# The first norm's weights as one row spread by TensorE, and the first row tile taken alone through all weight blocks

## The chip, the cores and the metric

The kernel runs on one NeuronCore of a Trainium2 chip. The metric is the device time of one launch in microseconds. The kernel before took 1310.49 us, the median of three runs (1310.32 to 1311.75). The engines go by the profile's names: PE is TensorE, DVE is VectorE, ACT is ScalarE, POOL is GpSimd, SP is SyncE, which issues most of the transfers.

## The reference

One layer of a decoder trunk over 1040 rows (16 learned meta tokens ahead of 1024 of the sequence), 1024 wide: a norm, a wide projection, an HGRN2 recurrence beside a causal pooling, a merge by gates, a projection, a residual, then a gated MLP with a causal convolution. Only its beginning matters here:

```python
def rmsnorm(x, gain):
    xf = x.astype(jnp.float32)
    y = xf * lax.rsqrt(jnp.mean(xf * xf, axis=-1, keepdims=True) + EPS)
    return (y * gain.astype(jnp.float32)).astype(x.dtype)
...
u = rmsnorm(h, mix_norm_pre[l])
proj = u @ w_in[l]
q, f_logit, i_in, g_out, v_pool, gate_a, gate_b = jnp.split(proj, cuts, axis=-1)
```

`i_in`, 512 columns wide, is the value input v of the recurrence. All is float32.

## The kernel before, in words

Every float32 operand of a large product is cut into a high part (a cast to the fast format float32r, on ScalarE) and a low part (operand less high part, on VectorE), and a product is three: high by high, high by low, low by high.

The opening computes v for nine row tiles: eight of 128 rows and one of the 16 meta tokens, in the order 1, 5, 2, 6, 3, 7, meta, 4, 8. This document numbers them by that order from 0. Four weight blocks of 256 x 512 (two k-steps of 128 each, so k = 0, 1 lie in block 0 and k = 6, 7 in block 3) hold the columns of `i_in`. They are loaded into `wiraw` and split once, by `split_wi`, into `whi`, `wlo` (`wihi`, `wilo` for the last). The steps of one row tile are:

- `norm_steps`: ScalarE squares the row with a sum and takes the root (`un`, `std`); VectorE takes the inverse (`rstd`) and then multiplies row, inverse and gains in two halves of 512 columns (L410). The gains `g1` must lie in all 128 partitions.
- `feature_steps`, once for each half: TensorE transposes four blocks of 128 x 128 into a PSUM bank `pt` (L421), ScalarE casts it to `uhi`, VectorE subtracts to `ulo`. The first half gives k = 0 to 3, the second k = 4 to 7.
- `v_mm`: three products for each k onto the tile's bank `pv` (L187 to L189), 128 x 512 each: 24 for a tile.

Before all that TensorE runs `warm(14)`, products of ones with the identity whose result nobody reads. A float32 product that isn't in the fast format shows in the trace as two instructions.

`manual_schedule` makes the written order the order of ScalarE, VectorE and TensorE in this part: each engine takes its instructions strictly in that order, so a waiting instruction holds up all behind it. SP and POOL take theirs in an order that a scheduler chooses; each load of SP also waits for the load eight before it. Tiles 0 and 1 are written out by hand; tiles 2 to 8 follow in a loop where `v_feat(i + 2)` and `v_norm(i + 4)` run ahead of the products.

`gain_bc` loads the gains into all partitions: one transfer of 512 KB that reads the same 4 KB row for each partition. On POOL, right after the identity and the ones, two kinds of masks for the heads are built: the base mask (`mtmp`, L573 to L580) and four level masks (`mt`, L583 to L591). They are first used some 330 us later.

Of the kernel before, what the change touches and what calls it, by code (L numbers as in the profile page):

```python
# [14 lines left out]
P = 128  # L15
# [54 lines left out]
def trunk_kernel(ctx: ExitStack, tc: tile.TileContext, x, meta_tokens, mix_norm_pre,  # L70
# [48 lines left out]
    def small(shape, name, tag, bufs=4):  # L119
        return sm.tile(shape, F32, tag=tag, name=nm(name), bufs=bufs)  # L120
# [7 lines left out]
    open_pool("ps", 8, PSUM)  # L128


    eps_t = const.tile([P, 1], F32, name="eps_t")
    dve.memset(eps_t, EPS)
    act.activation(small([P, 1], "std", "ns"), eps_t, AF.Sqrt)
    ident = const.tile([P, P], F32, name="ident")
    make_identity(nc, ident)
# [5 lines left out]
    def gain_bc(src, name):  # L141
        t = slot(D, name=name)
        nc.sync.dma_start(t, src[0].partition_broadcast(P))
        return t
# [304 lines left out]
    def load_wi(j):  # L449
        raw = slot(1024, name="wiraw")  # L450
        nc.sync.dma_start(raw.rearrange("p (k c) -> p k c", k=2), wblock(WIN, 2 * j, 2, CI, 512))
        return raw
# [1 line left out]

    vtiles = [row_tiles[i] for i in (1, 5, 2, 6, 3, 7, 0, 4, 8)]
    rows_in = [load_row(*vtiles[0])]
    g1 = gain_bc(mix_norm_pre, "g1")
    raws = [load_wi(0)]
    rows_in.append(load_row(*vtiles[1]))
    raws += [load_wi(j) for j in range(1, 4)]  # L460
    rows_in += [load_row(*rt) for rt in vtiles[2:]]

    prow = slot(P, name="prow")
# [106 lines left out]
    mbase = const.tile([P, SB], U8, name="mbase")  # L570
    mtmps = slot(P + len(LEVELS) * P // 2, name="mtmps")
    mtmp = mtmps[:, :P]
    pool_e.memset(mtmp, 1.0)  # L573
    pool_e.affine_select(out=mtmp, in_=mtmp, compare_op=ALU.is_ge, fill=0.0, base=0,
                         pattern=[[-2, P // 2], [0, 2]], channel_multiplier=1)
# [450 lines left out]
    vb = [bank("pv") for _ in range(2)]  # L1026
    E = mybir.EngineType
    with tc.manual_schedule(engines={E.Activation, E.DVE, E.PE}):
        warm(14)
        n0, n1 = (norm_steps(rows_in[i], P, g1) for i in range(2))  # L1030
        next(n0)
        next(n0)
        un0 = next(n0)
        f0 = feature_steps(un0, P, uhi, ulo, vtiles[0][0])
        split_wi(raws[0])
        next(f0)
        next(f0)
        next(f0)
        next(n1)
        next(f0)  # L1040
        next(n1)
        un1 = next(n1)
        v_mm(vb[0], vtiles[0][0], 0)
        v_mm(vb[0], vtiles[0][0], 1)
        split_wi(raws[1])
        f1 = feature_steps(un1, P, uhi, ulo, vtiles[1][0])
        next(f1)
        next(f1)
        split_wi(raws[2])
        next(f1)  # L1050
        next(f1)
        split_wi(raws[3])
        for i, j in ((0, 1), (1, 0), (0, 2), (1, 1), (0, 3), (1, 2), (1, 3)):
            for k in (2 * j, 2 * j + 1):
                v_mm(vb[i], vtiles[i][0], k)
        v_norm(2)
        v_norm(3)
        for i in range(2):
            v_feat(2 + i)
            v_norm(4 + i)  # L1060
        for i in range(2):
            v_out(vb[i], vtiles[i][0])
        for i in range(2, len(vtiles)):
            ps = bank("pv")
            for k in range(KD):
                v_mm(ps, vtiles[i][0], k)
            if i < 5:
                v_feat(i + 2)
            if i == 5:
                v_feat(7)  # L1070
                v_feat(8)
            v_norm(i + 4)
            if i == 3:
                params()
            if i == 5:
                for q in ("t2", "t1", "t3", "t4"):
                    two_halves(gq, q, NM)
                sums = [gate_steps(d) for d in ds]
            if i == len(vtiles) - 1:
                with tc.issue_after(loaded_row[-1].ins):  # L1080
                    gl = Loader([job("G", h)[:2] + (P,) for h in range(EARLY_G)])
            for j in SUMS_AT.get(i, ()):
                next(sums[j], None)
            v_out(ps, vtiles[i][0])
        gates.load_first(0)
        gates.load_first(1)
        gates.ahead(2)
        for h in range(EARLY_G):
            src, n_k, xs, chunks, post = job("G", h)
            r = proj(None, 0, n_k, xs, chunks, ws=gl.next(), name="pg", by_bank=2 * h)  # L1090
            if h == EARLY_G - 1:
                post(r)
            for j in SUMS_AT.get(9 + 2 * h, ()):
                next(sums[j], None)
            if h < EARLY_G - 1:
                post(r)
            if h == 0:
                dve.tensor_tensor(vm_hl[:NM], vm_hl[:NM], vm_low[:NM], ALU.add)
                nc.sync.dma_start(vmd, vm_hl[:NM])
                gates.load_first(2)  # L1100
                gates.ahead(4)
            for j in SUMS_AT.get(10 + 2 * h, ()):
                next(sums[j], None)

        close_pool("ps")
        open_pool("pf", 4, PSUM)
        gates.load_first(3)
        for e in range(0, EARLY, 2):
            p = gates.start_pair(e)
            for f in [f[i] for i in range(2) for f in p]:  # L1110
                f()
                for j in SUMS_AT.get(13, ()) if e == 0 else ():
                    next(sums[j], None)
# [701 lines left out]
```

## Time and profile before

| | |
|---|---|
| median of three runs | 1310.49 us |
| profiled execution | 1311.92 us |
| its span, first to last instruction | 1310.2 us |
| granted TensorE clock | 0.996 |
| TensorE busy | 1291.0 us, 99% of the span |
| VectorE, ScalarE, POOL busy | 963.7, 524.4, 355.4 us |

A row of a timeline reads: start and length in us from the span's start, engine, source line, operation, output and inputs by the program's names, partitions x elements, how many instructions were merged, and in brackets how long the engine had been idle and what ended that. In a row of windows the pairs in front of the clock are busy time and instructions of TensorE and of its weight loads. Ends of matmuls are modelled, so a length is longer than the distance to the next one.

### The profile page before, as it was taken

Reading aid. Unit: us, or ns where it says so; the run is one execution under the profiler, and the core shown is the slowest. Engines: PE = TensorE matmul, PEld = TensorE weight load, DVE = VectorE, ACT = ScalarE, POOL = GpSimd, SP = SyncE. Lnnn points to the kernel's source line nnn. Section 1 sums busy time; section 2 is a strip of 40 time slices with the busy share of each in tenths; the row PEclk is TensorE's granted clock in tenths of the full one; section 3 lists DMA queues with packets and bytes.
Section 4 is the critical chain, followed back from the end, with each engine's and each line's share of the span. In section 5 each row is a group of like instructions: output and inputs, shape, how many; then the busy total and the mean of one; then the engine's idle time right before and its main releaser. Section 6 shows DMA issues by size and latency. Waiting matters only on the chain.

```text
span 1310.2 us, 21958 instructions
## 1 busy us (share of the span) xinstructions
PE 1291.0 (99%) x8650; PEld 1139.6 (87%) x8650; DVE 963.7 (74%) x1296; ACT 524.4 (40%) x905; POOL 355.4 (27%) x307
## 2 busy tenths in 40 slices
PE   8999999999999898999999999999999999999998
PEld 7799899999999898978898888888888888888886
DVE  6768965454776877765588999888998985455758
ACT  5554533332245546236564222322222332444443
POOL 3015333130000000150045555553655652000000
PEclk9999999999999999999999999999999999999999
DMA  8135542325523776876677777658776799666644
GB/s 276 42 106 166 196 160 100 118 90 158 171 73 126 238 248 203 300 223 241 239 259 242 205 203 189 170 181 209 155 179 163 155 266 289 209 225 225 228 172 161
DMA packets 143801, 247.62 MB, mean 189 GB/s; under 512 B 11000, under 2 KB 75164, under 8 KB 143698
## 3 DMA queue, kind: packets, MB, share of 16 engines
q1 hardware_dynamic: 127026, 213.42, 48.7%
q0 software_dynamic: 12064, 24.38, 11.2%
q10 hardware_dynamic: 4608, 8.41, 1.7%
q8 instruction: 68, 1.11, 0.3%
q14 instruction: 35, 0.29, 0.1%
HBM read 174.11 MB, written 95.09 MB: 205 GB/s over the span
## 4 chain that ended last, share of the span: by engine, by line
PE 95%; ACT 2%; DVE 2%; DMA 1%; issue 1%; SPq 0%; DVEq 0%; ACTq 0%
PE P L307 17%; PE P L308 17%; PE P L310 17%; PE pd L187 5%; PE pd L189 5%; PE pd L188 5%; PE pm L187 2%; PE pm L188 2%; PE pm L189 2%; PE ppv L207 1%; PE ppv L211 1%; PE ppv L208 1%; PE pv L188 1%; PE pv L187 1%; PE pv L189 1%; PE pg L207 1%
## 5 line engine op out<-in xcount | busy, mean ns | idle before, releaser
L308 PE MATMUL P<-v,whi 128*128 128x512 f32 (+2 forms) x408 | 140.7, 353 | 0.0
L307 PE MATMUL P<-v,whi 128*128 128x512 f32 (+2 forms) x408 | 140.7, 352 | 0.0
L310 PE MATMUL P<-v,wlo 128*128 128x512 f32 (+2 forms) x424 | 135.1, 349 | 0.0
L278 POOL TENSOR_TENSOR swa<-wraw,wraw 128x512 f32<-128x512 f32 x32 | 49.2, 1539 | 192.1 <-DMA wraw<-in_ffn_w_gate_dram 73.9
L252 ACT CAST whi<-wraw 128x512 fp32r<-128x512 f32 x90 | 53.1, 618 | 102.2 <-PE P L308 87.2
L1525 DVE TENSOR_TENSOR rot<-wraw,rot 128x1024 fp32r<-128x1024 f32 x31 | 37.9, 1224 | 72.3 <-ACT rot L1524 72.3
L307 PEld LDWEIGHTS P<-v,whi 128*128 128x128 f32 x408 | 76.7, 188 | 10.5
L308 PEld LDWEIGHTS P<-v,whi 128*128 128x128 f32 x408 | 76.6, 188 | 10.2
L310 PEld LDWEIGHTS P<-v,wlo 128*128 128x128 f32 x424 | 74.0, 188 | 10.8
L189 PE MATMUL pd<-rot 128*128 128x512 f32 x274 | 82.5, 388 | 0.0
L188 PE MATMUL pd<-rot 128*128 128x512 f32 x274 | 82.5, 388 | 0.0
L187 PE MATMUL pd<-rot 128*128 128x512 f32 x274 | 81.9, 388 | 0.1
L253 DVE TENSOR_TENSOR wlo<-wraw,whi 128x512 fp32r<-128x512 f32 x86 | 74.4, 887 | 2.7 <-ACT whi L252 2.7
L252 ACT CAST whi<-swa 128x512 fp32r<-128x512 f32 x64 | 38.1, 619 | 90.3 <-PE P L308 79.9
L253 DVE TENSOR_TENSOR wlo<-swb,whi 128x512 fp32r<-128x512 f32 x64 | 65.5, 1030 | 8.9 <-ACT whi L252 8.7
L1524 ACT CAST rot<-wraw 128x1024 fp32r<-128x1024 f32 x31 | 32.7, 1054 | 90.8 <-PE pd L189 89.4
L307 PE MATMUL P<-uhi,whi 128*128 128x258 f32 (+2 forms) x240 | 68.5, 303 | 0.0
L308 PE MATMUL P<-ulo,whi 128*128 128x258 f32 (+2 forms) x240 | 68.4, 303 | 0.0
L252 ACT CAST whi<-swb 128x512 fp32r<-128x512 f32 x64 | 38.1, 618 | 70.8 <-PE P L308 57.9
L307 PE MATMUL P<-t4h,whi 128*128 128x258 f32 (+2 forms) x228 | 65.5, 304 | 0.0
L308 PE MATMUL P<-t4l,whi 128*128 128x258 f32 (+2 forms) x228 | 65.3, 304 | 0.0
L307 PE MATMUL P<-t2h,whi 128*128 128x258 f32 (+2 forms) x228 | 65.3, 304 | 0.1
(388 smaller groups left out, 3844.1 us busy)
## 6 DMA issues: line engine op xcount, KB each, us to landing
wraw<-in_w_in_dram SPq DMA_DIRECT2D x36, 512.0 KB, 4.6
yt<-ysum SPq DMA_DIRECT2D x33, 512.0 KB, 5.7
wraw<-in_ffn_w_gate_dram SPq DMA_DIRECT2D x26, 512.0 KB, 7.1
wraw<-in_ffn_w_up_dram SPq DMA_DIRECT2D x22, 512.0 KB, 5.2
wsum<-in_ffn_w_down_dram SPq DMA_DIRECT2D x22, 512.0 KB, 8.6
wraw<-in_w_out_dram SPq DMA_DIRECT2D x18, 512.0 KB, 4.3
ysum<-ys SPq DMA_DIRECT2D x11, 768.0 KB, 5.0
sa<-sscr SPq DMA_DIRECT2D x16, 513.0 KB, 5.7
```

Source lines behind the costliest of these rows:

```text
L187: pe.matmul(ps, ahi, bhi, start=first, stop=False)
L188: pe.matmul(ps, ahi, blo, start=False, stop=False)
L189: pe.matmul(ps, alo, bhi, start=False, stop=last)
L207: pe.matmul(ps[:, :n], whi[:, k, :], xhi, start=(k == 0), stop=False)
L252: act.copy(hi, src)
L253: (pool_e if 4 <= i < 2 * self.early else dve).tensor_tensor(lo, src, rr(hi), ALU.subtract)
L278: pool_e.tensor_tensor(s1, a21, a22, ALU.add)
L307: pe.matmul(d, whi[:, k, :], xh[:, c : c + w], start=(k == 0 and onto is None), stop=False, **go)
L308: pe.matmul(d, whi[:, k, :], xl[:, c : c + w], start=False, stop=False, **go)
L310: pe.matmul(x[:, o : o + w], wlo[:, k, :], xh[:, c : c + w], start=False, stop=(k == 3), **go)
L1524: act.copy(hi, src)
L1525: dve.tensor_tensor(lo, src, rr(hi), ALU.subtract)
```

## The change

The gains of the first norm are no longer loaded into all partitions. A single row of 4 KB is loaded by a transfer that ScalarE issues as its first instruction; two products of a column of ones with that row (128 x 512 each) put it into all partitions of two PSUM banks; VectorE copies the first half to `g1`, ScalarE the second. Three warm-up products stay of fourteen. SP's second load is now weight block 0, and weight block 1 goes ahead of tile 1's row.

The hand-written order of tiles 0 and 1 is another. Tile 0's second half of the norm follows its first products, and tile 0 goes through all four blocks before tile 1's first transposes; tile 1 then does four k-steps behind each of its halves.

On POOL the base mask begins with a copy of one element from `prow`, a tile of parameters loaded later, so that it is built after that load has landed; the level masks, which wait for nothing, then come first.

```diff
+    gain_row, ones_row = slot(D, name="grow"), slot(P, name="ones")
+    nc.scalar.dma_start(gain_row[:1], mix_norm_pre)
     eps_t = const.tile([P, 1], F32, name="eps_t")
     dve.memset(eps_t, EPS)
+    dve.memset(ones_row[:1], 1.0)
...
     rows_in = [load_row(*vtiles[0])]
-    g1 = gain_bc(mix_norm_pre, "g1")
-    raws = [load_wi(0)]
+    g1 = slot(D, name="g1")
+    raws = [load_wi(0), load_wi(1)]
     rows_in.append(load_row(*vtiles[1]))
-    raws += [load_wi(j) for j in range(1, 4)]
+    raws += [load_wi(j) for j in range(2, 4)]
...
     mtmp = mtmps[:, :P]
+    pool_e.tensor_copy(mtmp[:1, :1], prow[:1, :1])
     pool_e.memset(mtmp, 1.0)
...
-        warm(14)
+        warm(3)
+        gps = [bank("pg1") for _ in range(2)]
+        for j in range(2):
+            pe.matmul(gps[j], ones_row[:1], gain_row[:1, j * 512 : (j + 1) * 512], start=True, stop=True)
+        dve.tensor_copy(g1[:, :512], gps[0])
         n0, n1 = (norm_steps(rows_in[i], P, g1) for i in range(2))
         next(n0)
-        next(n0)
         un0 = next(n0)
+        split_wi(raws[0])
+        act.copy(g1[:, 512:], gps[1])
         f0 = feature_steps(un0, P, uhi, ulo, vtiles[0][0])
-        split_wi(raws[0])
         next(f0)
         next(f0)
+        for k in range(2):
+            v_mm(vb[0], vtiles[0][0], k)
+        next(n0)
+        split_wi(raws[1])
         next(f0)
-        next(n1)
         next(f0)
+        for k in range(2, 4):
+            v_mm(vb[0], vtiles[0][0], k)
+        split_wi(raws[2])
+        for k in range(4, 6):
+            v_mm(vb[0], vtiles[0][0], k)
         next(n1)
         un1 = next(n1)
-        v_mm(vb[0], vtiles[0][0], 0)
-        v_mm(vb[0], vtiles[0][0], 1)
-        split_wi(raws[1])
+        split_wi(raws[3])
+        for k in range(6, 8):
+            v_mm(vb[0], vtiles[0][0], k)
         f1 = feature_steps(un1, P, uhi, ulo, vtiles[1][0])
         next(f1)
+        next(n1)
         next(f1)
-        split_wi(raws[2])
+        for k in range(4):
+            v_mm(vb[1], vtiles[1][0], k)
         next(f1)
         next(f1)
-        split_wi(raws[3])
-        for i, j in ((0, 1), (1, 0), (0, 2), (1, 1), (0, 3), (1, 2), (1, 3)):
-            for k in (2 * j, 2 * j + 1):
-                v_mm(vb[i], vtiles[i][0], k)
+        for k in range(4, 8):
+            v_mm(vb[1], vtiles[1][0], k)
```

How that moves instructions is seen best on three stretches. The first is the start of TensorE's queue before (pt_225 and pt_232 are the halves of tile 0, pt_258 and pt_269 those of tile 1):

```order
L499 MATMUL pj_127<-ident,onesm_84 128x128 x14
L421 MATMUL pt_225<-ident,un_213 128x128 x4
L421 MATMUL pt_232<-ident,un_213 128x128 x4
L187 MATMUL pv_194<-whi_221,uhi_88 128x512
L188 MATMUL pv_194<-wlo_222,uhi_88 128x512
L189 MATMUL pv_194<-whi_221,ulo_89 128x512
L187 MATMUL pv_194<-whi_221,uhi_88 128x512
L188 MATMUL pv_194<-wlo_222,uhi_88 128x512
L189 MATMUL pv_194<-whi_221,ulo_89 128x512
L421 MATMUL pt_258<-ident,un_239 128x128 x4
L421 MATMUL pt_269<-ident,un_239 128x128 x4
```

And the same place now (pt_223 and pt_241 are the halves of tile 0):

```order
L502 MATMUL pj_130<-ident,onesm_88 128x128 x3
L1036 MATMUL pg_30_205<-grow_75,ones_76 128x512
L1036 MATMUL pg_31_206<-grow_75,ones_76 128x512
L424 MATMUL pt_223<-ident,un_211 128x128 x4
L190 MATMUL pv_198<-whi_218,uhi_92 128x512
L191 MATMUL pv_198<-wlo_219,uhi_92 128x512
L192 MATMUL pv_198<-whi_218,ulo_93 128x512
L190 MATMUL pv_198<-whi_218,uhi_92 128x512
L191 MATMUL pv_198<-wlo_219,uhi_92 128x512
L192 MATMUL pv_198<-whi_218,ulo_93 128x512
L424 MATMUL pt_241<-ident,un_211 128x128 x4
```

The gains' products stand ahead of all transposes, and tile 0's second half behind its first six products. Tile 1's first transposes come 18 products further down, behind the last product of tile 0. On VectorE the part of these two tiles was, before (whi_221, whi_254, whi_265 are weight blocks 0 to 2, wihi_276 is block 3; un_239 is tile 1):

```order
L410 SCALAR_TENSOR_TENSOR un_213<-row_90,rstd_217,g_8_92 128x512 x2
L509 TENSOR_TENSOR wlo_222<-wiraw_94,whi_221 128x1024
L426 TENSOR_TENSOR ulo_89<-pt_225,uhi_88 128x4x128
L399 RECIPROCAL rstd_243<-std_241 128x1
L426 TENSOR_TENSOR ulo_89<-pt_232,uhi_88 128x4x128
L410 SCALAR_TENSOR_TENSOR un_239<-row_96,rstd_243,g_8_92 128x512 x2
L509 TENSOR_TENSOR wlo_255<-wiraw_98,whi_254 128x1024
L426 TENSOR_TENSOR ulo_89<-pt_258,uhi_88 128x4x128
L509 TENSOR_TENSOR wlo_266<-wiraw_100,whi_265 128x1024
L426 TENSOR_TENSOR ulo_89<-pt_269,uhi_88 128x4x128
L509 TENSOR_TENSOR wilo_277<-wiraw_102,wihi_276 128x1024
```

And it is now (whi_218, whi_237, whi_254 and wihi_272 are the blocks, un_265 is tile 1):

```order
L413 SCALAR_TENSOR_TENSOR un_211<-row_94,rstd_215,g_10_96 128x512
L512 TENSOR_TENSOR wlo_219<-wiraw_97,whi_218 128x1024
L429 TENSOR_TENSOR ulo_93<-pt_223,uhi_92 128x4x128
L413 SCALAR_TENSOR_TENSOR un_211<-row_94,rstd_215,g_10_96 128x512
L512 TENSOR_TENSOR wlo_238<-wiraw_99,whi_237 128x1024
L429 TENSOR_TENSOR ulo_93<-pt_241,uhi_92 128x4x128
L512 TENSOR_TENSOR wlo_255<-wiraw_103,whi_254 128x1024
L402 RECIPROCAL rstd_269<-std_267 128x1
L413 SCALAR_TENSOR_TENSOR un_265<-row_101,rstd_269,g_10_96 128x512
L512 TENSOR_TENSOR wilo_273<-wiraw_105,wihi_272 128x1024
L413 SCALAR_TENSOR_TENSOR un_265<-row_101,rstd_269,g_10_96 128x512
```

Both tile 1's feature remainders (ulo of pt_282 and pt_302) now stand behind the last weight block, where one stood ahead of block 2 and one ahead of block 3. On ScalarE, before, from the first weight cast on:

```order
L508 CAST whi_221<-wiraw_94 128x1024
L424 CAST uhi_88<-pt_225 128x4x128
L424 CAST uhi_88<-pt_232 128x4x128
L405 ACTIVATE un_239,ssq_238<-row_96 128x1024
L397 ACTIVATE std_241<-ssq_238,eps_t 128x1
L508 CAST whi_254<-wiraw_98 128x1024
L424 CAST uhi_88<-pt_258 128x4x128
L508 CAST whi_265<-wiraw_100 128x1024
L424 CAST uhi_88<-pt_269 128x4x128
L508 CAST wihi_276<-wiraw_102 128x1024
```

And now:

```order
L511 CAST whi_218<-wiraw_97 128x1024
L1042 COPY g_10_96<-pg_31_206 128x512
L427 CAST uhi_92<-pt_223 128x4x128
L511 CAST whi_237<-wiraw_99 128x1024
L427 CAST uhi_92<-pt_241 128x4x128
L511 CAST whi_254<-wiraw_103 128x1024
L408 ACTIVATE un_265,ssq_264<-row_101 128x1024
L400 ACTIVATE std_267<-ssq_264,eps_t 128x1
L511 CAST wihi_272<-wiraw_105 128x1024
L427 CAST uhi_92<-pt_282 128x4x128
```

Weight blocks 1 and 2 now each stand behind a cast of tile 0's features, and tile 1's square and root stand between blocks 2 and 3. Far behind, in the heads, two remainders of weights and one sum of the pooling change places with their neighbours on VectorE and ScalarE; the rest of the program keeps its order.

## The prediction

> **What bounds the kernel now.** I read the page's first parts, then TensorE's waits in the first 120 us, then the timelines of the first 40 us. TensorE is busy for 99% of the span, so what counts is where it stands still. Up to 120 us that is only this (line, what ended the wait, us in total, times, longest):
>
> ```profile
> span 1310.2 us, 21958 instructions
> PE 1291.0 (99%) x8650; PEld 1139.6 (87%) x8650; DVE 963.7 (74%) x1296; ACT 524.4 (40%) x905; POOL 355.4 (27%) x307
> PE pj L499 <- POOL ident masks.py:199: 2.0, 1, 2.0
> PE pt L421 <- DVE un L410: 1.6, 2, 1.0
> PE pv L188 <- DVE wlo L509: 0.4, 2, 0.3
> ```
>
> Then it has no wait before the heads, 300 us on. So the end moves with the moment from which TensorE runs without a gap. Its timeline (start, length; the last row but one is the transposes of tiles 2 and 3, the last those of tile 5), and one row of the chain of waits for the pitch of a transpose:
>
> ```profile
> 2.03 5.67 PE L499 MATMUL pj<-ident,onesm 128*128 128x128 f32 x28 [2.03 <-POOL ident masks.py:199]
> 8.31 1.23 PE L421 MATMUL pt<-ident,un 128*128 128x128 f32 x8 [0.60 <-DVE un L410]
> 13.12 1.23 PE L421 MATMUL pt<-ident,un 128*128 128x128 f32 x8 [1.02 <-DVE un L410]
> 14.83 0.50 PE L188 MATMUL pv<-wlo,uhi 128*128 128x512 f32 x1 [0.25 <-DVE wlo L509]
> 24.26 1.91 PE L421 MATMUL pt<-ident,un 128*128 128x128 f32 x16
> 37.80 1.04 PE L421 MATMUL pt<-ident,un 128*128 128x128 f32 x8
> ...
> 24.42 1.75 PE pt L421 x16
> ```
>
> From 8.31 to 24.26 lie 15.95 us. The work in them is 48 products at 0.228 (24.26 − 14.83 holds 41 of them at that pitch) and 16 transposes at 0.109 (1.75 / 16): 12.7 us. So 3.3 us are gaps, all before 14.83; from there two tiles share each weight block, and VectorE stays ahead. The rows at 24.26 and 37.80 are my two marks.
>
> **The terms, from rows of VectorE, ScalarE and POOL:**
>
> ```profile
> 4.28 1.06 ACT L405 ACTIVATE un<-row 128x1024 f32<-128x1024 f32 x1 [1.98 <-DMA row<-in_x_dram]
> 5.46 0.29 ACT L397 ACTIVATE std<-ssq,eps_t 128x1 f32<-128x1 f32 x1
> 5.78 0.16 DVE L399 RECIPROCAL rstd<-std 128x1 f32<-128x1 f32 x1 [4.85 <-ACT std L397]
> 6.59 2.23 DVE L410 SCALAR_TENSOR_TENSOR un<-row,rstd,g 128x512 f32<-128x512 f32 x2 [0.64 <-DMA g<-in_mix_norm_pre_dram]
> 7.95 1.05 ACT L508 CAST whi<-wiraw 128x1024 fp32r<-128x1024 f32 x1 [2.19 <-DMA wiraw<-in_w_in_dram]
> 12.23 1.41 DVE L410 SCALAR_TENSOR_TENSOR un<-row,rstd,g 128x512 f32<-128x512 f32 x2
> 13.55 1.22 DVE L509 TENSOR_TENSOR wlo<-wiraw,whi 128x1024 fp32r<-128x1024 f32 x1
> 13.79 0.58 ACT L424 CAST uhi<-pt 128x512 fp32r<-128x512 f32 x1 [1.32 <-PE pt L421]
> 14.27 1.05 ACT L508 CAST whi<-wiraw 128x1024 fp32r<-128x1024 f32 x1
> 14.69 0.68 DVE L426 TENSOR_TENSOR ulo<-pt,uhi 128x512 fp32r<-128x512 f32 x1
> ```
>
> The next instruction of an engine starts about 0.1 before the recorded end (13.55 + 1.22 against 14.69), and a waiting engine starts 0.06 behind its releaser (wlo ends 14.77, the product starts 14.83). So on VectorE a weight remainder (wlo) takes 1.14, a feature remainder (ulo) 0.60, half a tile's multiplication (un) 0.67; on ScalarE a weight cast (whi) 0.96, a feature cast (uhi) 0.49 with 0.58 to its end, a tile's square and root some 1.4.
>
> **The gain row.** Removed is the 512 KB load: VectorE had its root's inverse at 5.94 and waited until 6.59. Without it SP's queue moves on: the first weight block landed some 3.7 us behind the row tile (7.95 − 4.28), of which 2.3 were the gain's (6.59 − 4.28), so now near 5.65, and the blocks behind it come 1.36 apart (7.95 − 6.59), tile 1's row, now behind block 1, at 8.3; ScalarE wants that row at 12.5. Added are a 4 KB load on ScalarE's queue, a fill on VectorE, two products and two copies. Issuing the load holds ScalarE's first work up by some 0.4 (SP's issue below), which the wait for the row until 4.28 hides; the fill (before 1 us) is hidden likewise. The load is bounded below by the quickest small one, above by the row tile issued at the same moment, which landed by 4.28:
>
> ```profile
> 0.81 0.38 SPq L444 DMA_DIRECT2D row<-in_x_dram  x1
> DMA to landing us min/median/max: 2.0/2.0/2.0
> 2.50:3.00 0.50, 0.50 (x4) 0.50 (x4) 1.00 0.76 311
> 6.50:7.00 0.50, 0.50 (x5) 0.50 (x5) 1.00 1.12 438
> 7.00:7.50 0.50, 0.50 (x7) 0.50 (x5) 1.00 1.04 422
> ```
>
> (The second row is the 32 KB copy into vm.) So 2.8 to 4.28; I take 3.4, when the three remaining warm-up products end (2.03 + 6 x 0.21; the last three rows count the warm-up's instructions: 4 or 5 in half a microsecond, 7 only from 7.0 on, though the granted clock reads 1.00). At that pitch a float32 product over 512 columns is two passes of 4 x 0.21, 1.7 us: first half of the gains 5.1 plus 0.2 to its end, second 6.8 plus 0.2. VectorE's copy of the first half (0.68, as ulo, which also reads PSUM) ends at 6.1, the inverse at 6.2. ScalarE's copy of the second stands behind the first weight cast (5.84 to 6.89) and ends at 7.67. So this part saves 0.4 us of 6.59, not the whole load.
>
> **The masks.** POOL's work on the base mask goes behind the load of prow. What it shared with the first multiplication (and prow's issue):
>
> ```profile
> 2.17 0.19 POOL L573 MEMSET mtmps<- 128x128 f32 x1
> 2.67 0.70 POOL L574 TENSOR_SCALAR_AFFINE_SELECT mtmps<-mtmps 128x128 f32<-128x128 f32 x1
> 4.51 0.70 POOL L576 TENSOR_SCALAR_AFFINE_SELECT mtmps<-mtmps 128x128 f32<-128x128 f32 x1
> 5.18 1.22 POOL L586 TENSOR_SCALAR_AFFINE_SELECT mtmps<-mtmps 128x64 f32<-128x64 f32 x4
> 6.66 0.86 POOL L589 TENSOR_TENSOR mtmps<-mtmps 128x32 f32<-128x32 f32 x4
> 7.49 0.78 POOL L579 TENSOR_TENSOR mtmps<-mtmps 128x32 f32<-128x32 f32 x1
> 13.32 0.36 SPq L470 DMA_DIRECT2D prow<-in_ffn_conv_w_dram  x1
> ```
>
> The two halves took 2.23 where the next pair takes 1.41: 0.82 lost while POOL ran its additions. The four level masks stay, and their additions come 1.5 us earlier (less 0.70 + 0.70 + 0.19, rows overlapping a little), eight of 0.21 from about 4.9 to 6.6; the multiplication starts at 6.2 amid them. Its loss lies between 0 and 0.82; I take 0.4, what is left of them. The base mask, now built after prow lands behind the rows queued ahead of it, some 17 to 21 us, is wanted only in the heads. If a select blocks VectorE there, that is up to 0.7, under VectorE's wait for tile 1's casts.
>
> The Trainium skill ("SBUF — State Buffer", section "SBUF: two separate sides") says that VectorE and GpSimd lock a shared port pair for one whole instruction and the loser blocks. By that a multiplication should lose one short POOL addition, about 0.2, so the sum would be +2.0 instead of +2.2; the row shows it losing to four in a row, and the row decides.
>
> **The order.** The multiplication ends near 7.4, so the first transposes come at 7.4 instead of 8.31: 0.9 gained. Then tile 0 alone goes through the four blocks, and nothing else is there for TensorE when a block is late:
> - ScalarE's cast of the first features ends 8.66, VectorE's wlo (behind whi) 8.52, ulo 9.40. Products of k = 0, 1 run from 8.7 to 10.4, with a gap of 0.3 for ulo. The transposes of the second half stand behind them, to 10.8; the cast of them ends 11.6.
> - Weight cast 2 stands behind that cast on ScalarE: 11.5 to 12.6. wlo of block 2 follows until 13.86. Products k = 4, 5 stand still from 12.9 to 13.9.
> - Then ScalarE does tile 1's square and root (to 14.1) ahead of weight cast 3 (to 15.04); wlo of block 3 ends 16.32. Products k = 6, 7 stand still from 15.3 to 16.4, and end at 17.5.
> - Tile 1's transposes are queued behind them. Each half pays transposes to cast to first product: 17.52 to 18.82, of which 0.44 is work, then 0.28 for ulo; twice. With 24 products and 8 transposes (6.3 us) tile 1 takes 8.6 us, to 26.2.
>
> In the old order both tiles' transposes came early and their casts lay under products. So the mark of 24.26 becomes 26.2. Tile 2 and 3's norms now come later too (ScalarE and VectorE start them at 23.0 instead of 16.6): VectorE's ulo of tile 2 stands behind tile 3's multiplications, and TensorE loses some 0.3 more before tile 2's products; the mark of 37.80 becomes 40.1. The same sums laid over the old order give 24.37 and 37.92 for the rows at 24.26 and 37.80, so they run 0.1 late, and I compare sums with sums: 40.12 − 37.92 = **+2.2 us**. By part: gain row and half the multiplication's loss −0.9 together (8.31 to 7.4), the order +3.1. Nothing later takes it back, since TensorE has no gap until the heads, whose waits are for work that follows it; a few rows of the heads change places (two remainders and a sum on VectorE), where no TensorE wait stood.
>
> **Sum.** The profiled run took 1311.92 us, with a span of 1310.2; +2.2 makes 1314.1, and the median of the runs, 1310.49, becomes **1312.7**, 0.17% more.
>
> **The rivals.**
> - *The gain row lands late* (18%; slower). TensorE's queue holds every transpose behind the two products. Past 3.4 each microsecond costs one: landing with the row at 4.28 gives +3.1, 1313.6. It exceeds 0.2% from 3.85 on. For it: it shares the engines with a row tile in flight. Against: 4 KB beside 512.
> - *The clock opens late* (12%; slower). In the rows above the pitch halves only after 4.9 us of unbroken products; now eleven warm-up products are gone, and a gap may stand ahead of the gains. A product then takes 0.43 instead of 0.228. Opened at 9.2 it gives +2.5, opened at 10.4 +3.0: 1313.5. The Trainium skill ("TensorE: Matmul & The Clock Gate", Part 1) has a free-running window of about 3.4 us that must be busy; by that the gains' 3.4 us of passes may just fill one or may straddle two. The rows before agree with a rise after sustained work, though none shows the window.
> - *The order costs nothing* (12%; within 0.2%): the casts and remainders keep up, and the 0.9 us gained at the first transposes is kept: 1309.6. Against it stand ScalarE's and VectorE's queues as summed above.
> - *VectorE never waits, and tile 1's casts are hidden* (5%; within 0.2%, to the fast side). From 7.4 VectorE has four wlo, two ulo, two halves of a multiplication and an inverse ahead of it, 7.3 us, so block 3 is ready no sooner than 14.7; seven products on, 16.3, and tile 1's 6.3 us of work make 22.6 at the first mark, −1.7: 1308.8. Even this best case falls short of 0.2%.
> - *The masks stay in the way* (part of the forecast's upper end): the full 0.82 is lost, as before: +2.6, 1313.1. Then that part doesn't do what it says.
>
> **How the numbers follow.** The forecast (+1.7 to +2.6) has 47%, the four rivals with chances 47%, and 6% are for something in the heads, half either way. About 0.2%, 2.6 us, is what a measurement of this kernel tells from no change. Slower by more: 18 + 12 + 3 of the heads and 2 of the forecast's edge, 35%. Faster by more: 3 of the heads and 1 of the fast rival, 4%. Within: 61%. The range runs from an order that costs only 0.5 (−0.4) to a late row, a late clock and the multiplication's whole loss together (2.2 + 0.9 + 0.8 + 0.4 = +4.3): 1310.1 to 1314.8.
>
> **What would show it.** First transposes near 7.4; gains' products from 3.4 in two stretches of 1.7; VectorE's first multiplication at 6.2, over 0.75 long; TensorE waiting for wlo twice for a microsecond in tile 0, tile 1's transposes near 17.5 with casts waited for twice; tile 2's transposes near 26.2, tile 5's near 40.1. It is wrong if tile 2's transposes stand before 24.3, or if the shift at 40 us isn't found at the end.

## The result, and the profile after

The changed kernel takes 1316.73 us, median of five runs (1315.31 to 1318.83), against 1310.28 us (six runs, 1309.84 to 1311.75) for the kernel before beside it: a ratio of 1.0046, 95% interval 1.0035 to 1.0058. It is slower by 4.6 to 7.6 us. The forecast was +2.2 us and a range up to 1314.8: the side was right, the size was not. Of the chances that were given, a kernel slower by more than 0.2% had 35%, one within 0.2% had 61%. (One more run, at a quarter less TensorE clock throughout, is left out of the median.) The profiled executions, 1311.92 before and 1316.73 after, differ by 4.8.

TensorE's timeline of the changed kernel; its lines lie 3 below those of the kernel before (L424 is the transposes, L190 to L192 the three products, L1036 the gains' products):

```profile
3.61 3.78 PE L1036 MATMUL pg<-grow,ones 1*128 1x512 f32 x4
7.46 1.09 PE L424 MATMUL pt<-ident,un 128*128 128x128 f32 x4
11.09 0.63 PE L191 MATMUL pv<-wlo,uhi 128*128 128x512 f32 x1
11.52 0.63 PE L192 MATMUL pv<-whi,ulo 128*128 128x512 f32 x1
13.37 0.39 PE L190 MATMUL pv<-whi,uhi 128*128 128x512 f32 x1
15.71 0.50 PE L191 MATMUL pv<-wlo,uhi 128*128 128x512 f32 x1 [0.76 <-DVE wlo L512]
19.31 0.60 PE L424 MATMUL pt<-ident,un 128*128 128x128 f32 x4
28.12 2.13 PE L424 MATMUL pt<-ident,un 128*128 128x128 f32 x16
41.91 1.03 PE L424 MATMUL pt<-ident,un 128*128 128x128 f32 x8
```

Up to 7.46 it goes as forecast. Then four cold transposes take 1.09 (0.60 at 19.31), and the products of the first features come 0.43 apart (11.09, 11.52) until about 12.3; only from there 0.23, and the length that the profile gives one falls from 0.63 to 0.39 (13.37). So TensorE ran its first features at half pitch. The two waits for a remainder in tile 0 (15.71 here, the other at 18.03) and those behind tile 1's transposes are there, each some 2 us later than forecast, and so are the two marks: 28.12 for 26.2, 41.91 for 40.1.

TensorE's waits up to 320 us (line, what ended the wait, us in total, times, longest; the warm-up's first wait and one of 0.2 for a cast are left out):

```profile
PE pv L190 <- ACT uhi L427: 2.0, 3, 0.7
PE pv L191 <- DVE wlo L512: 0.8, 1, 0.8
PE pv L191 <- DVE wilo L512: 0.7, 1, 0.7
PE P L310 <- ACT sg L629: 0.5, 1, 0.5
PE P L310 <- DVE sg L868: 0.4, 1, 0.4
PE P L310 <- DVE sg L866: 0.2, 1, 0.2
```

The three rows of `P` are new. They stand in the gates, at 94, 137 and 146 us, where the profile of the kernel before shows no wait and where the forecast said that none would come.

Where the time went is read best from one engine's instructions that are the same in both kernels. Three of ScalarE's, from its timeline of the kernel before:

```profile
87.62 0.46 ACT L625 ACTIVATE sg<-pg 128x342 f32<-128x342 f32 x1 [3.70 <-PE pg L189]
131.44 0.63 ACT L636 ACTIVATE fk<-sg 128x512 f32<-128x512 f32 x1 [6.15 <-DVE sg L862]
557.69 0.41 ACT L1132 CAST zc<-sa 128x256 fp32r<-128x256 f32 x1 [6.52 <-PE pba L211]
```

and the same three of the changed kernel:

```profile
91.79 0.46 ACT L629 ACTIVATE sg<-pg 128x342 f32<-128x342 f32 x1 [3.70 <-PE pg L192]
137.17 0.63 ACT L640 ACTIVATE fk<-sg 128x512 f32<-128x512 f32 x1 [6.37 <-DVE sg L866]
562.50 0.41 ACT L1148 CAST zc<-sa 128x256 fp32r<-128x256 f32 x1 [6.58 <-PE pba L214]
```

The shift is +4.17 when the opening is over, +5.73 at 131 us, the same at the end of the gates (a fourth instruction of the kind, 304.9 before and 310.64 after) and +4.81 behind the heads; it stays there to the end. (At 131 us ScalarE waits for VectorE, so the mark shows VectorE's delay: TensorE's own shift is 4.98 until 137 us and 5.73 from 146 us on.) This **shift at four marks** is what the experiments are read by: it says at which place a kernel wins or loses, and it doesn't mix the opening with the heads, where the profiled executions differ by up to 4 us for a reason of their own (last section).

### The profile page after: what moved, and what is told of

It reads as the page before. It is cut to its first block, busy times and chain, and to the rows that moved or that the text cites. A ratio compares the mean times of both kernels' runs of the same rounds, so it can differ in the third digit from the quotient of the medians.

```text
span 1315.0 us, 21925 instructions
## 1 busy us (share of the span) xinstructions
PE 1293.0 (98%) x8632; PEld 1136.6 (86%) x8632; DVE 968.0 (74%) x1298; ACT 525.4 (40%) x906; POOL 354.2 (27%) x308
## 4 chain that ended last, share of the span: by engine, by line
PE 92%; DVE 3%; ACT 3%; DMA 1%; issue 1%; POOL 0%; DVEq 0%; SPq 0%; ACTq 0%; POOLq 0%
PE P L310 16%; PE P L311 16%; PE P L313 16%; PE pd L190 5%; PE pd L191 5%; PE pd L192 5%; PE pm L190 2%; PE pm L191 2%; PE pm L192 2%; PE ppv L210 1%; PE ppv L214 1%; PE ppv L211 1%; PE pv L190 1%; PE pv L192 1%; PE pv L191 1%; PE pg L210 1%
## 5 line engine op out<-in xcount | busy, mean ns | idle before, releaser
L310 PEld LDWEIGHTS P<-v,whi 128*128 128x128 f32 x408 | 76.7, 188 | 10.4
L192 PE MATMUL pd<-rot 128*128 128x512 f32 x274 | 82.5, 388 | 0.0
L190 PE MATMUL pd<-rot 128*128 128x512 f32 x274 | 81.9, 388 | 0.1
```

What stands on the lines that cost most here:

```text
L190: pe.matmul(ps, ahi, bhi, start=first, stop=False)
L192: pe.matmul(ps, alo, bhi, start=False, stop=last)
L310: pe.matmul(d, whi[:, k, :], xh[:, c : c + w], start=(k == 0 and onto is None), stop=False, **go)
```

## The experiments

Shift of each profiled execution against that of the kernel before, in us, at these four instructions, and the time of all runs as a ratio with its interval:

| kernel | 87.6 | 131.4 | 304.9 | 557.7 | ratio, 95% interval |
|---|---|---|---|---|---|
| the changed kernel | +4.17 | +5.73 | +5.74 | +4.81 | 1.0046 (1.0035 to 1.0058) |
| a_rows128 | +2.15 | +2.68 | +2.86 | +0.99 | 1.0033 (1.0022 to 1.0045) |
| a_vb | +4.04 | +4.04 | +4.05 | +1.36 | 1.0038 (1.0024 to 1.0052) |
| a_rows128_vb | +2.14 | +2.84 | +2.84 | +1.66 | 1.0026 (1.0016 to 1.0036) |
| b_order | +4.00 | +3.99 | +4.02 | +0.01 | 1.0026 (1.0016 to 1.0037) |
| b_masks | +0.05 | -0.31 | -0.31 | -1.95 | 0.9996 (0.9987 to 1.0005) |
| b_warm3 | +0.80 | +0.92 | +1.08 | +2.05 | 1.0008 (0.9998 to 1.0018) |
| b_warm1row | +2.17 | +1.97 | +1.96 | +0.45 | 1.0003 (0.9994 to 1.0012) |
| b_warm32row | +1.03 | +1.00 | +1.02 | -0.13 | one run |
| b_warm64row | +0.87 | +1.15 | +1.16 | -0.39 | one run |
| c_best2 | +1.39 | +1.91 | +1.91 | +0.72 | 1.0009 (1.0000 to 1.0017) |
| c_best3 | -0.27 | +0.47 | +0.73 | -1.43 | 1.0004 (0.9993 to 1.0015) |
| c_best4 | +0.15 | +0.17 | +0.46 | +1.26 | 1.0001 (0.9992 to 1.0010) |

Names with a start from the changed kernel, with b from the kernel before, with c from both. The ratio's interval is 2 to 4 us wide; the causes below are told apart by the marks.

### Does the one-row form of the gains' products keep the clock shut?

**a_rows128.** The row of gains goes to the last of 128 partitions, ones fill the others, and the stationary matrix has a one in its last row alone:

```diff
-    nc.scalar.dma_start(gain_row[:1], mix_norm_pre)
+    nc.scalar.dma_start(gain_row[P - 1 : P], mix_norm_pre)
-    dve.memset(ones_row[:1], 1.0)
+    dve.memset(gain_row[: P - 1], 1.0)
+    dve.tensor_copy(ones_row, ident[:, P - 1 : P].to_broadcast([P, P]))
-            pe.matmul(gps[j], ones_row[:1], gain_row[:1, j * 512 : (j + 1) * 512], start=True, stop=True)
+            pe.matmul(gps[j], ones_row, gain_row[:, j * 512 : (j + 1) * 512], start=True, stop=True)
```

> The changed kernel, but the gains' products sum over all 128 rows (the gain row in the last row of a tile that is 1.0 elsewhere, and a stationary matrix with a one in its last row only): the same gains, the same number and width of products. Theory 1 (a product over one row does not keep TensorE's clock up, so the count of sustained work began anew at 7.46): the products of the first features come 0.23 apart from about 9.2 on, tile 2's transposes come at 26.2 instead of 28.12, and the run is 1.9 us shorter than the changed kernel: about +4 against the kernel before. Theory 2 (when the clock opens is chance): the marks scatter whatever the rows are. Theory 3 (the gaps between 7.46 and 12.4 hold the clock down): 28.1 again, +6.

TensorE's timeline:

```profile
7.18 0.63 PE L425 MATMUL pt<-ident,un 128*128 128x128 f32 x4
17.31 0.60 PE L425 MATMUL pt<-ident,un 128*128 128x128 f32 x4
26.09 2.15 PE L425 MATMUL pt<-ident,un 128*128 128x128 f32 x16
39.90 1.03 PE L425 MATMUL pt<-ident,un 128*128 128x128 f32 x8
```

Transposes at full pitch from 7.18 (four in 0.63), as are the products behind them, tile 2's transposes at 26.09, tile 5's at 39.90. Theory 1 holds; the clock costs 2.0 us (4.17 against 2.15). a_vb and a_rows128_vb, described further below, are a second such pair: the first four transposes take 1.09 with one row and 0.63 with 128. As the moment at which the clock opens may still differ by chance, the same question was put to the kernel before.

**b_warm3, b_warm1row, b_warm32row, b_warm64row.** The warm-up ahead of the opening is cut to three products, or kept at fourteen over 1, 32 or 64 rows (n below); nobody reads what it computes:

```diff
-        warm(14)
+        warm(3)
```
```diff
-            pe.matmul(junk_bank[:, :P], onesm, ident, start=True, stop=True)
+            pe.matmul(junk_bank[:, :P], onesm[:n], ident[:n], start=True, stop=True)
```

> The kernel before with 3 warm-up products instead of 14; nothing takes their place. Theory 1 (sustained work opens the clock after 4.9 us): the products that follow the transposes at 8.31 come 0.43 apart until about 13.2, the second transposes are slower, and tile 2's transposes come later than 24.26 by 0.5 to 2. Theory 2 (chance): the clock opens at any time, here and there at 7 as before. If the 14 are worth nothing: 24.3 and +0.

> The kernel before with its 14 warm-up products over one row of the ones and of the identity instead of 128; nothing else changes, they write to a bank that nobody reads. If one-row products do not open TensorE's clock, the products behind the transposes at 8.31 come 0.43 apart until about 12.1, as with 3 warm-up products, and tile 2's transposes come at 25.0 (+0.7). If any product opens it, the pitch is 0.23 from 9.6 on and tile 2's transposes come at 24.3 (+0). The run's time may move by up to 3 us either way with clock dips in the heads (440 to 450 and 520 to 528 us), so the verdict is read from the marks ahead of 400 us.

> The kernel before with its warm-up products over 32 rows. If the rows in use set what counts as activity and a quarter is too few, the pitch is 0.43 behind the transposes at 8.3 and tile 2's transposes come at 25 or later, as with one row. If only the one-row form is too little, the pitch is 0.23 from 9.6 on and tile 2's transposes come at 24.3.

> The kernel before with its warm-up products over 64 rows: the same two readings, 25 or later against 24.3. With the 32-row run it brackets where the clock opens, if it depends on the rows at all.

TensorE in b_warm1row, and then in b_warm64row:

```profile
2.03 6.34 PE L499 MATMUL pj<-ident,onesm 1*128 1x128 f32 x28 [2.03 <-POOL ident masks.py:199]
8.47 1.94 PE L421 MATMUL pt<-ident,un 128*128 128x128 f32 x8
17.44 0.63 PE L188 MATMUL pv<-wlo,uhi 128*128 128x512 f32 x1
26.36 1.91 PE L421 MATMUL pt<-ident,un 128*128 128x128 f32 x16
```

```profile
2.03 6.34 PE L499 MATMUL pj<-ident,onesm 64*128 64x128 f32 x28 [2.03 <-POOL ident masks.py:199]
8.30 1.96 PE L421 MATMUL pt<-ident,un 128*128 128x128 f32 x8
25.03 1.91 PE L421 MATMUL pt<-ident,un 128*128 128x128 f32 x16
```

Over 128 rows the 28 instructions of the warm-up took 5.67 and its last ones ran at full pitch; over 1, 32 or 64 rows they took 6.34 to the last at half pitch, and the transposes behind them, eight in 1.94 to 1.96 instead of 1.23, were cold. So six microseconds of unbroken products over 64 rows or fewer do not open the clock here; over 128 rows they do, some 5 us in. With one row it opened near 17.9, later than the 12.1 I expected, and ran on at half pitch through a stop at 13 us; with three full-row products (b_warm3) near 12.1. Tile 2's transposes stand at 26.36, 25.18 and 25.03 with 1, 32 and 64 rows and at 24.97 with three products, against 24.26; the price in the order of before is 0.8 to 2.2 us at 87.6.

Over all profiles: in the eight whose products ahead of the transposes use 128 rows throughout, the clock was open by 8.6; in the five with fewer rows it opened at 12 or later. Nothing between 64 and 128 rows was tried, and with the rows the number of operand values that aren't zero changes too; which of the two counts isn't told apart.

The Trainium skill ("TensorE: Matmul & The Clock Gate", Part 1) has a free-running activity window of about 3.4 us that must be busy. No run here shows the window itself. Behind the same transposes at 8.47 the clock was open by 14.0 with 32 rows and only at 17.9 with one row, which fits windows that lie otherwise in each execution, so the 1.1 us between these two need not come from the rows. That busy time over 64 rows doesn't count is not in the skill.

### What closes an open clock, and can the gain row be had with the old order?

**c_best2.** The hand order of the kernel before, the gains' products over 128 rows and in the banks `vb` (below), and on ScalarE the first block's cast ahead of the second copy of the gains:

```diff
         next(n0)
         next(n0)
+        wi.append(split_hi(raws[0]))
+        act.copy(g1[:, 512:], gps[1])
         un0 = next(n0)
         f0 = feature_steps(un0, P, uhi, ulo, vtiles[0][0])
-        split_wi(raws[0])
+        split_lo(raws[0])
```

> Both repairs, and the hand order of the kernel before (two tiles share each block), with the first block's cast ahead of the second copy of the gains on ScalarE. If order and gain row add, the shift at 80 us is 2.1 - 4.0 = -1.9 against the kernel before; if the order needed the slack that the gain row now takes, it lies between -1 and 0. The time: 0 to 2 us below the kernel before, which five rounds may or may not tell from the same.

It came out at +1.39. TensorE's row of the stop, and a view by windows of a microsecond (busy time and instructions, granted clock, share and rate of the DMA engines):

```profile
12.81 1.23 PE L425 MATMUL pt<-ident,un 128*128 128x128 f32 x8 [1.30 <-DVE un L414]
```

```profile
13.00:14.00 1.00, 1.00 (x9) 1.00 1.02 410
15.00:16.00 1.00, 1.00 (x4) 0.50 1.20 361
```

The clock had been open, and 1.8 us behind a stop of 1.3 us it shut, from some 14.6 to 18.0. The kernel before stops at the same place for 1.02 and stayed open.

**c_best3, c_best4.** Five products that nobody reads ahead of tile 1's transposes, into the warm-up's bank (the diff), or in c_best4 into `vb[1]`, tile 1's own bank, which is not begun yet:

```diff
         split_wi(raws[1])
+        warm(5)
         f1 = feature_steps(un1, P, uhi, ulo, vtiles[1][0])
```

> The kernel with both repairs and the order of before, plus 5 products into the unread bank ahead of tile 1's transposes, where TensorE stood idle from 11.4 to 12.8. If that idle time closed the clock from 14.6 to 18.0, the pitch stays 0.23 through, tile 2's transposes come at 23.5 (25.57 without the filling, 24.26 in the kernel before) and the shift at 80 us against the kernel before is -0.6, for 1 to 2 us less time than without the filling. If the idle time had nothing to do with it, the pitch doubles again for 3.4 us somewhere before 20 us and the mark is 25.5. The clock's window may lie otherwise in this execution, so one profile alone can show no doubling by luck; the times of all rounds stand beside it.

> The kernel with both repairs, the order of before and the 5 filling products, but these write to tile 1's own bank of values, which is not begun yet, instead of the warm-up's bank. If the 0.55 us wait at the change of PSUM pools came back with the filling because a bank stayed in use longer (any longer use of a bank shifts which bank the first pair behind the change takes), it goes again, and the shift against the kernel before stays at -0.3 from 80 to 110 us. If the wait depends on when the work reaches the change, it stays: +0.5 at 107 us. Behind that, 0.5 to 0.8 more if GpSimd's first addition of the next weights starts ahead of VectorE's scaling near 113 us, and none if behind it. The time: within 1 us of the kernel before.

TensorE in c_best3, and then its stop in c_best4:

```profile
10.80 1.28 PE L503 MATMUL pj<-ident,onesm 128*128 128x128 f32 x10
12.72 1.23 PE L425 MATMUL pt<-ident,un 128*128 128x128 f32 x8 [0.64 <-DVE un L414]
23.86 1.91 PE L425 MATMUL pt<-ident,un 128*128 128x128 f32 x16
```

```profile
13.16 1.23 PE L425 MATMUL pt<-ident,un 128*128 128x128 f32 x8 [1.17 <-DVE un L414]
```

Full pitch throughout, also in c_best4; tile 2's transposes at 23.86 (23.5 was expected) and 24.32. That the filling kept the clock open isn't shown by this: in c_best4 TensorE still stood 1.17 ahead of the transposes, little less than the 1.30 of c_best2 and more than the 1.02 of the kernel before, which stayed open without filling. One profile in which the clock shut can be chance, and the times of all runs don't tell the three kernels apart. What the two show is that with an open clock the gain row (with the masks' new place) is worth -0.27 to +0.15 at 87.6 in the old order, where -0.6 and -0.3 were expected: nothing. Neither kernel is faster than the one before (ratios 1.0004 and 1.0001), and the -1.9 that I had added up for c_best2 was wrong for another reason too: in the old order tile 1's transposes wait for VectorE (12.72 and 13.16 here, 13.12 before), whatever is gained ahead of them.

### The order by itself

**b_order.** The kernel before with the new order of tiles 0 and 1 alone; the gains come by the old load. The core of it (the rest is that of the change, without the copies of the gains):

```diff
-        v_mm(vb[0], vtiles[0][0], 0)
-        v_mm(vb[0], vtiles[0][0], 1)
...
-        for i, j in ((0, 1), (1, 0), (0, 2), (1, 1), (0, 3), (1, 2), (1, 3)):
-            for k in (2 * j, 2 * j + 1):
-                v_mm(vb[i], vtiles[i][0], k)
+        for k in range(6, 8):
+            v_mm(vb[0], vtiles[0][0], k)
+        f1 = feature_steps(un1, P, uhi, ulo, vtiles[1][0])
...
+        for k in range(4):
+            v_mm(vb[1], vtiles[1][0], k)
...
+        for k in range(4, 8):
+            v_mm(vb[1], vtiles[1][0], k)
```

> The kernel before with the hand order of the change alone: gains loaded as before, 14 warm-up products, masks as before. My theory of the order: tile 2's transposes come at 26.2 + 0.9 = 27.1 instead of 24.26, tile 5's at 41.0 instead of 37.80, and the run is 3.1 us longer than the kernel before, with TensorE's waits for a remainder in tile 0 and for the casts in tile 1. The rival (the order costs nothing): 24.3 and +0. The clock is open from 7 in this kernel under all theories.

One row of ScalarE and two of TensorE in b_order, and then TensorE in a_rows128_vb, which has the same order with the gain row:

```profile
10.70 1.05 ACT L508 CAST whi<-wiraw 128x1024 fp32r<-128x1024 f32 x1 [0.98 <-DMA wiraw<-in_w_in_dram]
15.52 0.50 PE L188 MATMUL pv<-wlo,uhi 128*128 128x512 f32 x1 [0.76 <-DVE wlo L509]
27.93 2.15 PE L421 MATMUL pt<-ident,un 128*128 128x128 f32 x16
```

```profile
13.73 0.50 PE L192 MATMUL pv<-wlo,uhi 128*128 128x512 f32 x1 [0.77 <-DVE wlo L513]
26.14 2.14 PE L425 MATMUL pt<-ident,un 128*128 128x128 f32 x16
```

The order costs 4.0 us, 0.9 more than expected, where the 512 KB load is still in the queue, and 2.0 to 2.4 where it isn't (2.14 against -0.27 and 0.15; the kernels without the load also have the base mask behind `prow` and the new order of loads, and these weren't run apart from the row in the new order). With the load, ScalarE stands 0.98 for block 1, the wait for block 2's remainder ends at 15.52 instead of 13.73, and every block is paid for, since tile 0 alone has nothing else to do.

### The two repairs together, and the two waits of the gates

**a_vb, a_rows128_vb.** The gains' products go into the two banks that hold the first values later; a_rows128_vb has the 128 rows besides.

```diff
-        gps = [bank("pg1") for _ in range(2)]
+        gps = vb
```

> The changed kernel with the gains' products in the two PSUM banks that the first values use later, instead of two banks of their own, so that the rotation of banks behind them is that of the kernel before. If the 0.55 us wait at 94 us comes from the rotation, it goes, and the shift against the kernel before is the same at 87 us and at 90 us, with a run 0.7 us shorter than the changed kernel. If it comes from the later start of the work ahead of it, it stays, and so does the time.

> The changed kernel with the gains' products over 128 rows and in the first values' own banks: both repairs at once. If clock and rotation are separate costs and all that was missing in the forecast, the shift against the kernel before is the forecast's +2.1 at 80 us and still +2.1 at 400 us, with no wait at the change of PSUM pools. If the repairs overlap, or something else grows behind 100 us, it is above 2.5 at 400 us.

The changed kernel's wait at the change of PSUM pools, where the program goes over from eight single banks to four pairs of banks (ScalarE's last sigmoid ahead of it, then TensorE's first product behind it), and the same product in a_vb:

```profile
93.69 0.46 ACT L629 ACTIVATE sg<-pg 128x342 f32<-128x342 f32 x1 [0.49 <-PE pg L192]
94.19 0.40 PE L310 MATMUL P<-uhi,whi 128*128 128x272 f32 x1 [0.55 <-ACT sg L629]
```

```profile
93.36 0.29 PE L310 MATMUL P<-uhi,whi 128*128 128x272 f32 x1
```

Without the two banks the wait is gone: the product is 4.87 behind the kernel before (89.32) in the changed kernel, where the shift was 4.17 ahead of it, and 4.04 in a_vb, where it was 4.04. With 0.1 more at the next product (4.98) the wait costs 0.8 us. The time of all runs is too coarse to show that (1.0038 against 1.0046). The wait was in both kernels with the added banks and in none without, save c_best3, where the warm-up's bank stays in use until 12 us; c_best4, which uses another bank for the same products, has none. So it is the number and length of bank uses in the opening that decides, 80 us later, whether the first product takes a bank that ScalarE is still reading. That the banks themselves go round in such a way is inferred; no view shows a bank's number.

a_rows128_vb has +2.14 at 87.6 as expected, and no such wait, but +2.84 at 131 us, where I had hoped for +2.1. What differs from the kernel before in between lies at 114 to 117 us. VectorE's scaling and GpSimd's first addition of the next weights, in the changed kernel and in a_vb:

```profile
116.83 1.29 POOL L281 TENSOR_TENSOR swa<-wraw,wraw 128x512 f32<-128x512 f32 x1 [3.25 <-DMA wraw<-in_w_in_dram]
116.95 1.47 DVE L642 TENSOR_SCALAR fk<-fk,oml,lb 128x528 f32<-128x528 f32 x1 [0.71 <-ACT fk L640]
```

```profile
116.00 0.56 DVE L642 TENSOR_SCALAR fk<-fk,oml,lb 128x528 f32<-128x528 f32 x1 [0.71 <-ACT fk L640]
116.20 1.51 POOL L281 TENSOR_TENSOR swa<-wraw,wraw 128x512 f32<-128x512 f32 x1 [3.56 <-DMA wraw<-in_w_in_dram]
```

Whichever starts first has its usual length. GpSimd came first in the changed kernel, a_rows128, a_rows128_vb and c_best2, and VectorE took 1.43 to 1.52; VectorE came first in the ten others, the kernel before among them, and took 0.56. The starts are 0.1 to 0.7 apart, the one set by a landing load, the other by TensorE. Behind it TensorE loses 0.75 us in the changed kernel (4.98 ahead of it, 5.73 behind), 0.7 in a_rows128_vb and 0.5 in c_best2, and nothing in a_rows128. How much of that comes from the 0.9 by which VectorE was late isn't settled. TensorE's waits for VectorE's sums stand 20 to 30 us later, in the changed kernel at 137.28 (0.19) and 146.21 (0.37), and b_warm64row, where VectorE came first, has one like the second and loses 0.28 by it:

```profile
146.21 0.36 PE L310 MATMUL P<-t2h,whi 128*128 128x272 f32 x1 [0.37 <-DVE sg L868]
```

```profile
141.63 0.36 PE L307 MATMUL P<-t2h,whi 128*128 128x272 f32 x1 [0.34 <-DVE sg L864]
```

No run changed this meeting alone. The Trainium skill ("SBUF — State Buffer", section "SBUF: two separate sides") says that the two engines share a pair of ports, that a VectorE instruction in a two-port mode, or with two inputs in SBUF, competes with GpSimd for it, and that whichever starts first has it for its whole instruction while the other blocks. These rows agree in who loses, VectorE 0.9 to a GpSimd addition of 1.29; no view shows in which mode VectorE's scaling runs.

### The masks

**b_masks.** The kernel before with the base mask behind the load of `prow`:

```diff
     mtmp = mtmps[:, :P]
+    pool_e.tensor_copy(mtmp[:1, :1], prow[:1, :1])
     pool_e.memset(mtmp, 1.0)
```

> The kernel before with the base mask built behind the load that the change puts it behind; gains and order as before. If POOL's additions slow VectorE's first multiplication (2.23 us for its two halves, 1.41 for a later pair), the two halves now take 1.4 to 1.8 and the first transposes come 0.4 to 0.8 earlier than 8.31, of which TensorE keeps less at tile 2's transposes, where tile 0's wait for a block follows: -0.4 to 0. If something else slows it (the gain's load landing in two pieces), it stays 2.2. Nothing is expected in the heads.

VectorE's first multiplication and TensorE's transposes of tiles 0 and 2:

```profile
6.66 1.46 DVE L410 SCALAR_TENSOR_TENSOR un<-row,rstd,g 128x512 f32<-128x512 f32 x2 [0.60 <-DMA g<-in_mix_norm_pre_dram]
7.60 1.23 PE L421 MATMUL pt<-ident,un 128*128 128x128 f32 x8 [0.25 <-DVE un L410]
24.22 1.91 PE L421 MATMUL pt<-ident,un 128*128 128x128 f32 x16
```

1.46 instead of 2.23, as POOL's additions are over by 6.50: they were the cause, and moving them brings the first transposes forward by 0.7. Tile 2's keep 0.04 of it, as in the cases above. That this kernel is 0.31 ahead at 131 us has no cause here, and what the masks do to the heads can't be told from their scatter (last section).

## Why the prediction was right or wrong, by its own steps

- **The opening up to the first transposes** was right in its number, 7.46 for 7.4, but in part by luck. The gains' products began 0.2 late and took 1.9 each for 1.7. VectorE's multiplication came 0.3 later than the 6.2 of the forecast and so lost nothing to POOL, whose eight additions (4.91 to 6.49) were over: its first half took 0.79, its second, later, 0.74. The late start and the loss that didn't come cancel. And the transposes show no wait for VectorE, whose first half ended at 7.31: what they stood behind was the gains' products, which ended at 7.39 and not at 7.0 as forecast.
- **The order** stalled as described: both waits for a remainder, tile 1's casts waited for twice. With the clock open the whole queue sum is hit: tile 1's transposes at 17.31 (forecast 17.5), tile 2's at 26.09 (26.2), tile 5's at 39.90 (40.1), +2.15 at 87.6 us (+2.2). Its division was loose: "order +3.1, gain row -0.9" are not two numbers that add. The order costs 4.0 with the old load and 2.0 to 2.4 with the new; the row, with the masks, is worth 1.9 in the new order (4.00 against 2.14) and nothing in the old one.
- **The clock rival, at 12%, was the true case, and under-priced.** I let the clock open by 10.4 and so at most 0.8 us more; it opened at 12.3 and cost 2.0. I asked whether there would be a gap ahead of the gains' products. There was none to speak of, and they still didn't count, since they use one row. This is the step that failed first: the forecast counted the gains' 3.4 us of products as work that replaces the warm-up, and its sum put the loss of the eleven warm-up products at nothing. Measured, it is 2.0 us. The Trainium skill ("TensorE: Matmul & The Clock Gate", Part 1) led me the same way: by its window alone the one-row products could have served.
- **"Nothing later takes it back, since TensorE has no gap until the heads"** failed too. It holds of b_order, which is as late and loses nothing there (4.00 at 87.6, 4.02 at 304.9), but not of a kernel with two more banks: 0.8 us at the change of PSUM pools. Another 0.75 went at the two waits for VectorE behind its meeting with POOL; why these came is only in part shown.
- **Sum.** 2.15 + 2.0 + 0.8 + 0.75 = 5.7, the shift from 131 to 305 us. The profiled runs end 4.8 apart because the profiled execution of before lost more clock in its heads; the medians lie 6.5 apart, and the 0.8 beyond 5.7 is within the interval and has no cause of its own here.
- The rivals of a late row (it was there by 3.61), of an order that costs nothing and of a VectorE that never waits fell.

## What to carry to other kernels

Before warm-up work is replaced by useful work, look at its shape and not only at its length: the time at half pitch is seen in the distance between products, and it stayed 0.43 behind six microseconds of products over 1, 32 or 64 rows. A forecast that takes the waits ahead of a point for the whole loss should still ask what stands just barely in time behind it (a bank freed half a microsecond early, two engines that start within 0.2 us), for a shift or an added buffer can turn such a place. And terms that are measured on the same bottleneck don't add: gain row and order were worth 1.9 and 4.0 with one partner and 0 and 2.2 with the other.

## What the runs showed of the hardware that I had not expected

- The granted clock reads 1.00 in the profile while the cold start runs at half pitch, so it doesn't show the very thing that cost most here; a clock that shuts again later does show, as 0.50.
- It shuts again in the heads too. The kernel before, by windows of 4 us:

```profile
436.00:440.00 4.00, 2.20 (x11) 1.00 0.85 275
440.00:444.00 4.00, 3.95 (x16) 0.57 1.05 371
518.00:522.00 4.00, 1.73 (x10) 1.00 0.52 177
522.00:526.00 4.00, 4.00 (x16) 0.57 0.83 204
```

  Behind two stretches where TensorE stands for 1.8 and 2.3 of 4 us the clock is halved for some 3.4 us (440.4 to 443.9 and 522.3 to 525.7 by the distance of the products), 1.7 us lost each time. The changed kernel's profile has one such place, those of b_order, a_rows128, a_vb, a_rows128_vb and c_best3 none. This is part of what the last two marks of the table differ by, and part of why runs of one kernel scatter over 4 us: it is decided anew in each execution. Behind a stop of 1.3 us the clock shut in c_best2; behind stops of 1.4 and 1.8 in the heads of a_rows128 it did not.
- Whether filling the heads' stops, as c_best3 does in the opening, would win this time back was not tried.
